# Eight feed-forward modulation chunks: from matmuls to ScalarE scalings summed by adding transfers

## The chip, the core and the metric

The kernel runs on one core of a Trainium2 chip. The metric is the device time of one launch in microseconds; less is better. The kernel before takes 1097.15 us (median of three runs, 1096.75 to 1098.19). A core has TensorE (matmul, PE; its weight loads are PEld), VectorE (DVE), ScalarE (ACT), GpSimd (POOL) and SyncE (SP), each with its own queue of instructions that it runs in order, and 16 DMA engines that move data when one of the queues issues a transfer. They meet at semaphores only.

## The reference

One transformer layer on a sequence of 256 tokens with 2048 features: windowed grouped-query attention with a sink, then a squared-ReLU MLP, each wrapped in an adaptive LayerNorm. What matters here is the modulation: one vector `c` of 2048 numbers gives all shifts, scales and gates.

```python
c_act = jax.nn.silu(c)
mod = c_act @ mod_w[i] + mod_b[i]
sh_m, sc_m, g_m, sh_f, sc_f, g_f = jnp.split(mod, 6, axis=-1)
...
hff = x * (1.0 + sc_f[:, None, :]) + sh_f[:, None, :]
y = sq_relu_mlp(hff, mlp_w1[i], mlp_b1[i], mlp_w2[i], mlp_b2[i])
x = layer_norm(DEEPNORM_ALPHA * x + (1.0 + g_f[:, None, :]) * y, ln_mlp_g[i], ln_mlp_b[i])
```

`c_act @ mod_w` is a vector times a matrix: 2048 x 12288 weights in f32, 100 MB, each used once. Everything is computed to nearly f32 accuracy.

## The kernel before

**Weights.** All large weights come through one stream, class `Stream`. Its list `q` is filled in program order by `S.plan`. Each entry is a load of 128 x 2048 f32 (1 MB) into a buffer called `raw`, issued on SyncE (L202). While attention starts there are eight `raw` buffers; from the second step of the projection loop on there are five (`RAWS`). A load whose buffer is still in use waits at the head of SyncE's queue, and all later loads wait behind it. A matmul weight is split into a high half `wh` (cast by ScalarE, L247) and a low half `wl` (subtraction on VectorE, L218), 1024 columns at a time, five buffers of each. The product is then three matmuls: L498, L499, L500 in the attention part, L971 to L973 in the first feed-forward stage.

**Modulation.** Class `Mod` computes one group of columns of `c_act @ mod_w`. An entry of the stream that belongs to a `Mod` is a chunk, and its work is `Mod.step`. For the feed-forward scale and shift (`m_ff`) there are four groups, 0 to 3, of eight chunks each, 32 chunks in all. A chunk holds two rows of blocks (`k` = 0, 1); each is 128 x 1024, and `cact[:, kt]` has the 128 values of `c_act` that go with its partitions. A chunk is done in one of two ways:

- on TensorE (`quad`, L307): four matmuls side by side in the four column groups of the array, with `c_act` as the weight, f32, 256 columns each, per `k`. They add up in the PSUM tile `pm`, of which there is one.
- on VectorE (`dve`, L343 and L345): multiply by `c_act` and add into an SBUF tile `part` of 128 x 1024. At the end of the group (`Mod.end`) a further `quad` with ones as weights sums `part` over the partitions into the same `pm`.

`Mod.end` then copies `pm` to `mrow` (L361). `columns` transposes `mrow` (L377) to a scale and a shift per feature, and `ff_columns` (L885 to L887) merges them with the LayerNorm's gain. In group 1 chunks 1, 4, 5, 6 are on VectorE, in group 2 chunk 2 alone, in group 3 six of eight; the others are on TensorE.

**Stages.** Around the change: (1) attention by head groups (scores L687 and L693, softmax L702 to L717, transposes L728, values L743) with the output projection (`project`, matmuls L498 to L500, VectorE L803 to L810 and L751 to L753) in a loop of 21 steps; the chunks of `m_ff` 0, 1 and the first two of 2 are mixed in by `SLOT_FILL`. (2) After the last projection the LayerNorm: statistics (L753, L757), `norm_scalars` (L759 to L767), `normed` (L780 on ScalarE, L782 on VectorE), then transposes L901 and the modulated input of the MLP, `ff_input` (L907, L910, L913, L915). `S.vecs(4)` takes four chunks of group 2 here. (3) The first feed-forward stage: 16 steps over `w1a`, with the rest of groups 2 and 3 mixed in by `W1_FILL`; steps 1, 7 and 9 ask for the columns of groups 1, 2 and 3. (4) The other hidden blocks and the output, to the end.

**Order.** A planner (the Tile framework) orders the instructions of every engine: it goes through them by program order as priority, with its own estimate of when inputs arrive, and lets an instruction whose inputs are due pass one whose inputs are not. It also places tiles into buffers and adds all waits. The tile pool `gen` has 20 buffers of 128 x 1024, tag `g4`; `part` comes from there. While `S.behind` is set (stage 1), the first matmul of a `quad` is kept behind the last projection or attention matmul that came before it in the program.

**GpSimd's transfers.** GpSimd issues the broadcast of a bias (`bias_all`, L170), the gate rows (`gate`, L393 and L396) and the loads of `x` (L868).

Of the kernel before, what the change touches and what calls it, by code (L numbers as in the profile page):

```python
# [14 lines left out]
AF = mybir.ActivationFunctionType  # L15
OP = mybir.AluOpType
# [16 lines left out]
FFG = (4, 4, 4, 4)  # L33
# [15 lines left out]
def hybrid_kernel(ctx: ExitStack, tc: tile.TileContext, a, out: bass.AP):  # L49
    nc = tc.nc  # L50
# [23 lines left out]
    def g4(dt=F32):  # L74
        return gen.tile([128, 1024], dt, tag="g4", name="g4")
# [14 lines left out]
    onesf = cst.tile([128, 128], F32, name="onesf")  # L90
# [12 lines left out]
    cact = cst.tile([128, NK], F32, name="cact")  # L103
# [70 lines left out]
    class Stream:  # L174
# [4 lines left out]
        def __init__(self):  # L179
            self.q, self.raw = [], []  # L180
            self.hs, self.ls, self.src = [], [], []
            self.free, self.home, self.used = [raws] * RAWS + [raws2] * MORE, [], 0
            self.of = []
            self.deep = True
            self.at = self.im = 0
            self.nh, self.nl = NHIGH, NLOW
            self.stop = 0
            self.pace = VECS
            self.pin = self.behind = False
            self.prev = None  # L190
            self.side = {}
# [91 lines left out]


    class Mod:
        def __init__(self, srcs, width, dve=(), bias=None):
            self.srcs, self.dve, self.bias = srcs, set(dve), bias
            self.pairs = width == 64
            self.w = 128 if self.pairs else width
            self.kc = 2048 // (4 * width)  # L290
            self.n = NK // self.kc
            self.i = self.planned = 0
            self.whole = len(self.dve) == NK
            self.first = True
            self.part = None
            self.start = -1 if bias is None else max(min(dve) - 1, 0)
# [18 lines left out]
        def step(self, raw):  # L315
            w, kc, i = self.w, self.kc, self.i
            if i == 0 and not self.whole:
                self.ps = psm.tile([128, 512], F32, name="pm")
            r = raw.rearrange("p (k j n) -> p k j n", k=kc // 2 if self.pairs else kc, j=4)
            self.i += 1  # L320
            last = self.i == self.n
            if i == self.start:

                if not self.whole:
                    self.part = [g4() for _ in range(2)]
                for n, p in enumerate(self.part):
                    nc.gpsimd.memset(p, 0.0)
                    nc.scalar.dma_start(p[0:1], self.bias[:, n * 1024:n * 1024 + 1024])
            for k in range(kc):
                kt = i * kc + k  # L330
                if self.pairs:
                    if k % 2 == 0:
                        cols = [cact[:, kt + j // 2:kt + j // 2 + 1].to_broadcast([128, 32]) for j in range(4)]
                        self.quad(cols, [r[:, k // 2, j] for j in range(4)], last and k == kc - 2)
                elif i in self.dve:
                    e = min(4 * w, 1024)
                    new = self.part is None
                    if new:
                        self.part = [g4() for _ in range(4 * w // e)]
                    for n, p in enumerate(self.part):  # L340
                        s = raw[:, k * 4 * w + n * e:k * 4 * w + n * e + e]
                        if new:
                            nc.vector.tensor_scalar(p[:, :e], s, cact[:, kt:kt + 1], None, op0=OP.mult)  # L343
                        else:
                            nc.vector.scalar_tensor_tensor(p[:, :e], s, cact[:, kt:kt + 1], p[:, :e],  # L345
                                                           op0=OP.mult, op1=OP.add)
                else:
                    stop = last and k == kc - 1 and not self.dve
                    self.quad(cact[:, kt:kt + 1].to_broadcast([128, 32]), [r[:, k, j] for j in range(4)], stop)
            if last and not self.whole:  # L350
                self.end()

        def end(self):
            w = self.w
            per = 1024 // w
            if self.dve:
                self.quad(onesf[:, :32], [self.part[j // per][:, (j % per) * w:(j % per) * w + w]
                                          for j in range(4)], True)
            self.r = sml.tile([128, 512], F32, name="mrow", bufs=2)
            if self.bias is None:  # L360
                nc.scalar.copy(self.r[:, :w], self.ps[:, :w])  # L361
            else:
                nc.scalar.activation(self.r, self.ps, AF.Identity, bias=onesf[:, 0:1])
# [32 lines left out]
            nc.gpsimd.dma_start(g[h], row[:, h * 1024:h * 1024 + 1024].partition_broadcast(128))  # L396
        return lambda c: g[c // 2][:, (c % 2) * 512:(c % 2) * 512 + 512]

    def groups(src, sizes, dves):
        out, c0, k0 = [], 0, 0  # L400
        for nk, dve in zip(sizes, dves):
            n = 2 * nk
            out.append((Mod([src[c0 + i] for i in range(n)], 64 * nk, dve), k0, nk))
            c0 += n
            k0 += nk
        return out

    m_mix = groups(a["modm"], MIXG, [(), (), (), (1, 3, 4, 6), (1, 3, 4, 6), (1, 3, 4, 6)])
    m_ff = groups(a["modf"], FFG, [(1, 3, 5, 7), (1, 4, 5, 6), (2,), (1, 2, 4, 5, 6, 7)])
    m_gm = Mod([a["modgm"][i] for i in range(NK)], 512, (1, 3, 5, 6, 8, 9, 11, 12, 14), a["modgmb"])  # L410
    m_gf = Mod([a["modgf"][i] for i in range(NK)], 512, range(NK), a["modgfb"])

# [23 lines left out]
    for g in range(2, G):  # L436
        n = len(ORDER[g])
# [54 lines left out]
    acc, xts, held, xs = {}, {}, {}, [None] * 4  # L492
# [70 lines left out]
    def qkv(g, ch):  # L563

        _, k0, nk = m_mix[g]
        hh, hl = held[g]
        wh, wl = S.main()
        per = 4 // nk
        for ci in range(per):
            p = ch * per + ci  # L570
            c = CORD[p]
            go_on, held_back = c in half, ((g, ch), p) in CARRY
            pss = half.pop(c, None) or banks()
            for k2 in range(0, nk, 2):
                for t in range(NT):
                    for k in (k2, k2 + 1):
                        s = slice(k * 256 + t * 128, k * 256 + t * 128 + 128)
                        mm3(pss[t], hh[:, s], hl[:, s], wh(ci * nk + k), wl(ci * nk + k),
                            k == 0 and not go_on, k == nk - 1 and not held_back)
                S.done()  # L580
                if per == 1 and k2 == 0:
                    yield
            if held_back:
                half[c] = pss
            else:
                evict(c, pss)
            if per == 2 and ci == 0:
                yield
# [195 lines left out]
    def project(j, c):  # L784
        wh, wl = S.main()
        oh, ol = oT[j]
        pss = [psa.tile([128, 512], F32, name="pa") for _ in range(NT)]
        last = j == 3 and c == 3
        for t, rs in [(0, range(4)), (1, range(4))] if last else [(t, (r, r + 1)) for r in (0, 2) for t in range(NT)]:
            for r in rs:  # L790
                s = slice(t * 512 + r * 128, t * 512 + r * 128 + 128)
                mm3(pss[t], oh[:, s], ol[:, s], wh(r), wl(r), r == 0, r == 3)
            if t == 1 or last:
                S.done(not last)
            if last:
                add_gated(pss[t], t, c, g1, st)
                sc.append(norm_scalars(st[t]))
                normed(0, t)
            if t == 1 and rs[0] == 0:
                yield  # L800
        for t, ps in enumerate(pss):
            if j == 0:
                nc.vector.tensor_add(part(ys, t, c), ps, bo(c))  # L803
            elif j < 3:
                y = part(ys, t, c)
                nc.vector.tensor_add(y, y, ps)
                if j == 2:
                    z = part(xs, t, c)
                    nc.vector.tensor_mul(y, y, g1(c))
                    nc.vector.scalar_tensor_tensor(z, z, ALPHA, y, op0=OP.mult, op1=OP.add)  # L810
            elif not last:
                add_gated(ps, t, c, g1, st)
# [21 lines left out]
    for n in range(21):  # L834
        j, i = n // 4, n % 4
# [9 lines left out]
        if n + 1 < len(LATE):  # L845
            w = qkv(*LATE[n + 1])
        else:
            if n == 5:
                ys, bo = [g4b() for _ in range(4)], bias_all(a["bo"], [g4b(), g4b()])
            w = project((n - 5) // 4, (n - 5) % 4)  # L850
# [13 lines left out]
        if n == 9:  # L864

            for c in range(4):
                xs[c] = g4()
                i = nc.gpsimd.dma_start(xs[c].rearrange("p (t n) -> p t n", t=NT), a["x"][:, :, 512 * c:512 * c + 512])  # L868
# [86 lines left out]
    for n, (kg, fq) in enumerate(W1A):  # L955
# [4 lines left out]
        for fp in range(2):  # L960
# [3 lines left out]
            for fi in range(2):  # L964
                o = ps[:, fi * 256:fi * 256 + 256]
                for k in range(4):
                    w = (fp * 2 + fi) * 4 + k
# [208 lines left out]
```

## Time and profile before

| What | Value |
|---|---|
| median of three runs | 1097.15 us |
| the profiled execution's own time | 1100.0 us |
| its span, first to last instruction | 1098.2 us |
| granted clock of TensorE | 0.991 |
| busy: TensorE, VectorE, ScalarE, GpSimd | 1067.6, 804.2, 522.0, 30.0 us |
| DMA queue of SyncE (q1): moved, share of the engines | 279.85 MB, 66.9% |
| DMA queue of GpSimd (q0): moved, share | 10.50 MB, 2.7% |

How to read the lines that follow. A line of a group has the source line, engine, operation, out<-in by the program's names, shapes, and after the bar the busy time, the mean in ns, and the idle time just before with what ended it. A line of the chain has start, length and what ran. Matmuls overlap in the pipeline, so one matmul's duration (392 ns) is longer than its step in a row of them (about 230 ns). An f32 matmul of `quad` is recorded as two instructions.

### The profile page before, as it was taken

To read this page: it belongs to the slowest core of one execution; us is meant where nothing else is said; L and a number is where in the kernel's file an instruction comes from. 1 tells how busy PE (TensorE), PEld (TensorE's weight loads), DVE (VectorE), ACT (ScalarE), POOL (GpSimd) and SP (SyncE) were. 2 spreads that over 40 slices of the span, in tenths; PEclk is the share of its full clock that TensorE was granted. 3 is DMA by queue.
4 is the path that set the end of the run, shared out by engine and by line. 5 is a ranking of instruction groups with operands and counts; after the bars stand their busy time and mean duration, and the time that the engine had idled before them with its cause. 6 is when DMAs were issued, how large, how long until landed. Compare 5 with 4: busy or idle time off the path is not lost.

```text
span 1098.2 us, 15487 instructions
## 1 busy us (share of the span) xinstructions
PE 1067.6 (97%) x6098; PEld 863.1 (79%) x6098; DVE 804.2 (73%) x1162; ACT 522.0 (48%) x806; POOL 30.0 (3%) x54
## 2 busy tenths in 40 slices
PE   8889999998999999999999999999999999999995
PEld 6657677665677799988888888888888888888884
DVE  4597899978899877754588889756666557665676
ACT  5333346765673537643344543344453334544340
POOL 1000000001000000000000010001000000000001
PEclk9989999999999999999999999999999999999998
DMA  9999987789985996555578788866555555557511
GB/s 384 425 427 425 427 357 280 271 297 379 377 315 201 361 360 244 185 192 192 195 301 303 272 313 306 312 220 225 184 189 190 197 196 186 178 185 267 191 75 77
DMA packets 43337, 292.70 MB, mean 267 GB/s; under 512 B 5104, under 2 KB 5232, under 8 KB 9472
## 3 DMA queue, kind: packets, MB, share of 16 engines
q1 hardware_dynamic: 39312, 279.85, 66.9%
q0 software_dynamic: 3200, 10.50, 2.7%
q10 hardware_dynamic: 752, 1.35, 0.3%
q8 instruction: 48, 0.79, 0.3%
q14 instruction: 25, 0.20, 0.0%
HBM read 289.57 MB, written 2.11 MB: 266 GB/s over the span
## 4 chain that ended last, share of the span: by engine, by line
PE 86%; DVE 7%; DMA 4%; ACT 2%; issue 1%; DVEq 0%; ACTq 0%
PE pa L995 16%; PE pa L500 15%; PE pa L498 15%; PE pa L499 15%; PE pa L996 8%; PE pa L972 3%; PE pa L971 3%; PE pa L973 3%; PE pm L307 3%; DVE wl L218 2%; DMA raw<-in_modm 2%; DMA raw<-in_modf 1%; DVE g L345 1%; DMA raw<-in_wqkv 1%; PE pa L687 1%; PE pa L743 1%
## 5 line engine op out<-in xcount | busy, mean ns | idle before, releaser
L218 DVE TENSOR_TENSOR wl<-raw,wh 128x1024 fp32r<-128x1024 f32 x332 | 403.9, 1223 | 223.6 <-ACT wh L247 222.9
L247 ACT CAST wh<-raw 128x1024 fp32r<-128x1024 f32 x332 | 347.1, 1051 | 441.3 <-PE pa L500 228.6
L498 PE MATMUL pa<-wh,g 128*128 128x512 f32 x816 | 324.1, 398 | 5.1 <-ACT g L519 2.6
L500 PE MATMUL pa<-wh,g 128*128 128x512 f32 x816 | 318.9, 392 | 4.1 <-DVE g L521 3.0
L499 PE MATMUL pa<-wl,g 128*128 128x512 f32 x816 | 320.0, 392 | 0.0
L995 PE MATMUL pa<-g,wh 128*128 128x512 f32 x768 | 270.1, 397 | 0.0
L996 PE MATMUL pa<-g,wl 128*128 128x256 f32 x768 | 214.9, 280 | 0.0
L498 PEld LDWEIGHTS pa<-wh,g 128*128 128x128 f32 x816 | 153.9, 189 | 46.8 <-issue 7.5
L500 PEld LDWEIGHTS pa<-wh,g 128*128 128x128 f32 x816 | 153.5, 188 | 41.2 <-DVE g L521 6.0
L499 PEld LDWEIGHTS pa<-wl,g 128*128 128x128 f32 x816 | 153.9, 189 | 33.0 <-issue 2.4
L995 PEld LDWEIGHTS pa<-g,wh 128*128 128x128 f32 x768 | 144.2, 188 | 36.0 <-issue 0.8
L996 PEld LDWEIGHTS pa<-g,wl 128*128 128x128 f32 x768 | 144.8, 189 | 0.1
L345 DVE SCALAR_TENSOR_TENSOR g<-raw,cact,g 128x1024 f32<-128x1024 f32 x65 | 82.6, 1280 | 2.8 <-DMA raw<-in_modf 2.3
L972 PE MATMUL pa<-g,wh 128*128 128x256 f32 x256 | 72.7, 285 | 0.4 <-DVE g L915 0.4
L971 PE MATMUL pa<-g,wh 128*128 128x256 f32 x256 | 72.5, 286 | 0.0
L973 PE MATMUL pa<-g,wl 128*128 128x256 f32 x256 | 72.3, 283 | 0.0
L307 PE MATMUL pm<-raw,cact 128*32 128x256 f32 (+2 forms) x776 | 48.8, 375 | 5.9 <-DMA raw<-in_modf 3.2
L971 PEld LDWEIGHTS pa<-g,wh 128*128 128x128 f32 x256 | 48.8, 192 | 1.3 <-issue 0.8
L972 PEld LDWEIGHTS pa<-g,wh 128*128 128x128 f32 x256 | 49.1, 192 | 0.9 <-DVE g L915 0.8
L973 PEld LDWEIGHTS pa<-g,wl 128*128 128x128 f32 x256 | 49.1, 192 | 0.0
L345 DVE SCALAR_TENSOR_TENSOR g4b<-raw,cact,g4b 128x1024 f32<-128x1024 f32 x32 | 40.7, 1280 | 9.0 <-DMA raw<-in_modgf 8.8
L307 PEld LDWEIGHTS pm<-raw,cact 128*32 128x32 f32 x776 | 20.9, 112 | 25.9 <-issue 11.5
(165 smaller groups left out, 741.6 us busy)
## 6 DMA issues: line engine op xcount, KB each, us to landing
raw<-in_w SPq DMA_DIRECT2D x64, 1024.0 KB, 4.9
raw<-in_w1b SPq DMA_DIRECT2D x48, 1024.0 KB, 5.0
raw<-in_modm SPq DMA_DIRECT2D x32, 1024.0 KB, 14.8
raw<-in_modf SPq DMA_DIRECT2D x32, 1024.0 KB, 6.9
raw<-in_wqkv SPq DMA_DIRECT2D x24, 1024.0 KB, 12.8
raw<-in_modgm SPq DMA_DIRECT2D x16, 1024.0 KB, 7.5
raw<-in_wo SPq DMA_DIRECT2D x16, 1024.0 KB, 7.5
raw<-in_w1a SPq DMA_DIRECT2D x16, 1024.0 KB, 7.6
```

Of the source, the lines that this page charges most:

```text
L218: self.pinned(nc.vector.tensor_sub(l, r, f32(self.hs[n])))
L247: self.pinned(nc.scalar.copy(h, s))
L307: i = nc.tensor.matmul(self.ps[32 * j:32 * j + 32, :w], lhsT[j] if type(lhsT) is list else lhsT, rhs[j], start=self.first, stop=stop)
L345: nc.vector.scalar_tensor_tensor(p[:, :e], s, cact[:, kt:kt + 1], p[:, :e], op0=OP.mult, op1=OP.add)
L498: nc.tensor.matmul(ps, xh, wh, start=start, stop=False)
L499: nc.tensor.matmul(ps, xh, wl, start=False, stop=False)
L500: S.prev = nc.tensor.matmul(ps, xl, wh, start=False, stop=stop).ins
L971: nc.tensor.matmul(o, wh(w, 128), hh, start=new, stop=False)
L972: nc.tensor.matmul(o, wh(w, 128), hl, start=False, stop=False)
L973: nc.tensor.matmul(o, wl(w, 128), hh, start=False, stop=end)
L995: nc.tensor.matmul(ps, wh(k, 128), hb, start=k == 0, stop=False)
L996: nc.tensor.matmul(ps[:, :256], wl(k, 128), hb[:, :256], start=False, stop=k == NK - 1)
```

## The change

Beside `dve`, a group can now have a set `acc` of chunks. For such a chunk ScalarE multiplies each 128 x 1024 half by its `c_act` column. The first half of a group goes into a new SBUF tile `sum` (from `gen`). Every later one is scaled in place in its `raw` buffer, and GpSimd issues a transfer from `raw` to `sum` that adds to what is there. At the end of the group one more `quad` with ones sums `sum` over the partitions into `pm`. Group 1's chunks 0, 2, 3 and group 2's chunks 0, 1, 3, 4, 5 are done so: eight chunks, sixteen halves, fourteen transfers. They were all on TensorE before. Group 1 keeps chunk 7 on TensorE, group 2 keeps 6 and 7.

```diff
-        def __init__(self, srcs, width, dve=(), bias=None):
-            self.srcs, self.dve, self.bias = srcs, set(dve), bias
+        def __init__(self, srcs, width, dve=(), bias=None, acc=()):
+            self.srcs, self.dve, self.bias, self.acc = srcs, set(dve), bias, set(acc)
+            self.sum = None
...
+                elif i in self.acc:
+
+                    s = raw[:, k * 1024:k * 1024 + 1024]
+                    if self.sum is None:
+                        self.sum = g4()
+                        nc.scalar.activation(self.sum, s, AF.Copy, scale=cact[:, kt:kt + 1])
+                    else:
+                        nc.scalar.activation(s, s, AF.Copy, scale=cact[:, kt:kt + 1])
+                        nc.gpsimd.dma_start(self.sum, s, accum_op=OP.add)
...
-                    stop = last and k == kc - 1 and not self.dve
+                    stop = last and k == kc - 1 and not self.dve and not self.acc
...
-                                          for j in range(4)], True)
+                                          for j in range(4)], not self.acc)
+            if self.acc:
+                self.quad(onesf[:, :32], [self.sum[:, j * w:j * w + w] for j in range(4)], True)
...
-    def groups(src, sizes, dves):
+    def groups(src, sizes, dves, accs=((),) * 8):
...
-    m_ff = groups(a["modf"], FFG, [(1, 3, 5, 7), (1, 4, 5, 6), (2,), (1, 2, 4, 5, 6, 7)])
+    m_ff = groups(a["modf"], FFG, [(1, 3, 5, 7), (1, 4, 5, 6), (2,), (1, 2, 4, 5, 6, 7)],
+                  [(), (0, 2, 3), (0, 1, 3, 4, 5), ()])
```

More of the change, by code (lines that the diff above doesn't have):

```diff
@@ L397, in gate @@
         return lambda c: g[c // 2][:, (c % 2) * 512:(c % 2) * 512 + 512]
-    def groups(src, sizes, dves):
+    def groups(src, sizes, dves, accs=((),) * 8):
         out, c0, k0 = [], 0, 0
-        for nk, dve in zip(sizes, dves):
+        for nk, dve, acc in zip(sizes, dves, accs):
             n = 2 * nk
-            out.append((Mod([src[c0 + i] for i in range(n)], 64 * nk, dve), k0, nk))
+            out.append((Mod([src[c0 + i] for i in range(n)], 64 * nk, dve, acc=acc), k0, nk))
             c0 += n
```

## The prediction

> **What bounds the kernel now.** I read the page first (busy times, then the chain that ended last), then the stages around the changed chunks.
>
> ```profile
> PE 1067.6 (97%) x6098; PEld 863.1 (79%) x6098; DVE 804.2 (73%) x1162; ACT 522.0 (48%) x806; POOL 30.0 (3%) x54
> PE 86%; DVE 7%; DMA 4%; ACT 2%; issue 1%; DVEq 0%; ACTq 0%
> ```
>
> TensorE holds 86% of the chain, so work taken off it counts, where it is really the last to finish. The table by stretch (columns: us; busy and instructions of PE, PEld, DVE, ACT, POOL; granted clock; DMA share and GB/s) follows the feed-forward chunks through the attention and projection stage (281 to 358.3), the LayerNorm gap (358.3 to 366.5) and the first feed-forward stage.
>
> ```profile
> 281.00:300.00 19.00, 18.98 (x134) 12.26 (x135) 16.30 (x32) 14.78 (x37) 0.00 (x0) 1.00 0.92 357
> 300.00:320.00 20.00, 20.00 (x134) 13.56 (x130) 19.80 (x42) 14.26 (x37) 1.10 (x2) 1.00 0.91 347
> 320.00:340.00 20.00, 20.00 (x109) 14.54 (x106) 17.34 (x32) 11.14 (x23) 0.00 (x0) 1.00 0.64 245
> 340.00:358.30 18.30, 18.30 (x82) 15.08 (x82) 17.56 (x25) 5.44 (x6) 0.00 (x0) 1.00 0.48 172
> 358.30:366.50 8.20, 7.07 (x99) 3.52 (x97) 6.96 (x29) 2.65 (x6) 0.00 (x0) 1.00 0.83 296
> 366.50:415.00 48.50, 48.10 (x413) 45.54 (x410) 38.22 (x51) 24.86 (x35) 0.00 (x0) 1.00 0.96 384
> 281.00:358.30 77.30, 77.28 (x450) 55.42 (x449) 70.99 (x130) 45.62 (x101) 1.10 (x2) 1.00 0.74 282
> ```
>
> From 281 to 358.3 TensorE is busy without a break, VectorE is close behind (70.99 of 77.30), ScalarE has 31.7 us free. The DMA engines are nearly full until 320 and half idle after it. In the gap TensorE is not the bound; after it, it is again.
>
> **What is removed.** Count the groups of feed-forward modulation from 0. Group 1's chunks 0, 2, 3 and group 2's 0, 1, 3, 4, 5 leave TensorE. The chain shows what one chunk costs there (x16 is one chunk: two halves of four matmuls, each recorded twice; the x24 is chunk 7 of group 1 with the closing sum over `part`).
>
> ```profile
> 281.90 1.00 PE pm L307 x16
> 287.86 1.00 PE pm L307 x16
> 292.86 1.00 PE pm L307 x16
> 311.15 1.43 PE pm L307 x24
> 316.36 1.00 PE pm L307 x16
> 338.95 1.00 PE pm L307 x16
> ```
>
> Chunks 0, 2, 3 of group 1 and 0, 1 of group 2 stand at 281.90, 287.86, 292.86, 316.36 and 338.95: five times 1.00, all on the path, -5.00 us. The x24 prices a closing sum: 1.43 - 1.00 = 0.43 us. The other three chunks of group 2 run in the gap:
>
> ```profile
> 357.15 1.14 DVE wl L218
> 358.31 4.93 DMA raw<-in_modf
> 363.28 1.05 PE pm L307 x10
> 364.33 0.37 PE pt L901 x2
> 364.69 0.57 PE pm L307 x8
> 365.26 0.49 PE pt L901 x3
> 365.78 0.57 ACT g L907
> ```
>
> There the chain is VectorE, then the load of the last chunk of group 2, then the transposes L901, which need the normalised rows anyway. Three chunks more or less on TensorE before 363.28 change nothing: 0. An earlier load could give up to the 1.05 that stands before the transposes; I take 0, as they also need the LayerNorm chain.
>
> **What is added on TensorE.** A second closing sum in each of the two groups, 0.43 each. Group 1's is on the path (+0.43). Group 2's follows the last chunk around the transposes (+0.43).
>
> **What is added on ScalarE.** Sixteen scalings of 128x1024: two write the sum, fourteen work in place. The nearest rows, of ScalarE over the stage and of the end:
>
> ```profile
> L247 ACT CAST wh<-raw 128x1024 fp32r<-128x1024 f32 x17 | 17.7, 1050 | 19.3 <-PE pa L500 12.0 <-DVE g L752 7.2
> L717 ACT ACTIVATE g<-g,rs 128x256 f32<-128x256 f32 x20 | 8.6, 505 | 1.0 <-DVE rs L711 1.0
> L1080 ACT ACTIVATE g<-g,r 128x512 f32<-128x512 f32 x2 | 1.4, 723 | 5.5 <-DVE r L767 5.5
> ```
>
> L717 and L1080 are the same operation with a scale per partition: 505 ns at 256 columns, 723 at 512, so 218 per 256, and 723 + 436 = 1.16 us at 1024 (the cast's 1.05 is the other end). Sixteen make 18.6 us. If fourteen fall into the stage (16.2), they lie in its 31.7 free, in pieces: the casts L247 had waited 12.0 us for buffers that TensorE frees, so a cast 1.16 us late still is ahead. I charge 0. Without that cover, a cast that TensorE waits for would cost up to 1.16 per scaling.
>
> **What is added on GpSimd and the DMA engines.** Fourteen transfers from SBUF into SBUF that add, 512 KB each, five for group 1 and nine for group 2. Each waits for its scaling and, since all of a group write one tile, for the transfer before it. GpSimd's issues of this size cost 0.55 us, 7.7 in all, on an engine busy 1.10 us of the stage. Queued on GpSimd with them are the loads of x ahead and two bias loads, which are first used in the feed-forward output. The trace has no transfer that adds. The nearest are GpSimd's 512 KB loads:
>
> ```profile
> L170 POOL DMA_DIRECT2D g4b<-in_b x2: 547/548/549, 311.4 to 319.3; - x2
> DMA to landing us min/median/max: 4.3/5.5/6.8
> L396 POOL DMA_DIRECT2D g4b<-row x4: 532/547/562, 245.5 to 748.4; - x4
> DMA to landing us min/median/max: 4.3/6.6/8.7
> g<-in_x POOLq DMA_DIRECT2D x4, 512.0 KB, 11.1
> ```
>
> The ends are 4.3 and 8.7 (11.1 where four stand in one queue); I take 5.5, as most of group 2's run after 320, where the share falls to 0.64 and 0.48. Group 1: five make 27 us. Its chunk 0 can be scaled when it lands, not when TensorE reaches it: the loads from 264.20 below. Done by about 305, before its closing sum at 312 less what is saved: hidden, 0. Group 2 is tighter:
>
> ```profile
> 264.20 10.10 SPq L202 DMA_DIRECT2D raw<-in_modf  x3
> 332.78 8.87 SPq L202 DMA_DIRECT2D raw<-in_modf  x4
> DMA to landing us min/median/max: 4.7/5.7/7.7
> ```
>
> The four from 332.78 are its chunks 3 to 6 (the landing row is of SyncE's loads in the stage). With 3.57 us saved by then, chunk 3 is issued at 329.2, lands at 334.9, is scaled at 336.1, and six transfers follow in a row: with 5.5 they end at 369.1. The closing sum can wait, because the planner orders each engine by when inputs are due, and its columns are asked for only at step 7 of the first feed-forward stage; I price it at 0 and the other case as a rival. The Trainium skill ("DMA: Bandwidth & Descriptors", section "Anatomy of one DMA — SWDGE (gpsimd) path") gives such a transfer about 2.0 us plus bytes over 436 GB/s. That would be 3.2 us here, the six would end at 355 and the rival below would fall away; the rows, all 4.3 and above, do not agree.
>
> **A raw buffer is now held** until its second transfer has landed, not until TensorE has read it. Five buffers serve all loads, and SyncE's queue stands still behind a load whose buffer is not free. Chunks that ScalarE takes when they land start their holding earlier, so I charge 0, with 0 to 13 us as bounds (third rival).
>
> **VectorE as the next bound.** If TensorE needs 77.30 - 4.57 = 72.73, VectorE's 70.99 fill 98% of it. Where they already touched:
>
> ```profile
> PEld pa L498 <- DVE g L345: 0.8, 1, 0.8
> PEld pa L498 <- DVE wl L218: 0.3, 1, 0.3
> ```
>
> That is 1.1 us in the stage before; I charge as much again, +1.1, with 0 and 4.57 (everything taken) as the ends.
>
> **The sum.** -5.00 + 0.43 + 0.43 + 1.1 = -3.0 us. The profiled execution took 1100.0 us (span 1098.2), so it would take 1097.0. It stood 2.85 above the median of 1097.15; against that median the forecast is 1094.1. Its own range is 1091.6 (no VectorE loss, and the 1.05 before the transposes won) to 1095.5.
>
> **Rivals.**
> 1. VectorE takes the gain. The four windows of the stage show 1.0, the third 2.7 us free; if the order of its work keeps the 6.3 idle us that it has, nothing is won and the closing sum remains: 1097.15 + 0.43 = 1097.6. For it speaks 19.80 of 20 us from 300 to 320; against it, that the high and low halves are made several buffers ahead of TensorE.
> 2. Slower, by one wait: the closing sum of group 2 stands in TensorE's order before the transposes of the gap while its transfers still run. Its place is 364.69 less the 4.6 saved, 360.1. Six transfers from 336.1 reach it if each takes more than 4.0 us. At 4.3 it waits 1.8; at 5.5, 9.0, which makes 1094.1 + 9.0 = 1103.1; at 6.6, 15.6. Against it: nothing needs this sum for another 40 us, so it is placed there only if the planner takes the transfers for shorter than they are.
> 3. The adding transfers slow the weight loads. At 357 GB/s for a share of 0.92 a full load is 388 GB/s; one add occupies the engines 1.35 us if its 0.52 MB count once, 2.7 if twice. Six before 320 are 8 to 16 us, where 3.3 are free, so loads come 5 to 13 us later; the 17 us free after 320 then take up the rest. If the cover of casts ahead is 5 us short, the sum is 1094.1 + 5 = 1099.1 and, at the far end, 1102. The Trainium skill ("Collectives: The Full Stack", section "The bandwidth ceiling: the fold count and why AG ≠ RS ≠ AR") says that an add in a transfer needs two source reads on one ring, which halved the rate there. That speaks for the 2.7 and against the change; no run here shows it yet.
>
> **How the numbers follow.** 0.2% of 1097 is 2.2 us, about what can be told from no change. The forecast 0.50, of which 0.02 falls within 2.2; VectorE 0.15 (no difference); the wait at the closing sum 0.22 (slower); the loads 0.13 (slower). Faster 0.48, same 0.17, slower 0.35. The range runs from 1091.6 to 1103.1, which leaves out the waits over 9 us and the far end of the loads, under 2 in 10.
>
> **What would show it.** L307 on TensorE: 128 instructions fewer, 16 more on the sum. Between 281 and the end of the projection TensorE without gaps and about 4.5 us shorter. Sixteen scalings of about 1.16 us, most right after their loads land. Fourteen transfers on GpSimd, 4.3 to 6.6 us each, one after another. No wait of TensorE for a transfer at a closing sum. The gap after the projection as long as before. I am wrong if TensorE idles before the closing sum of group 2 (rival 2), if casts wait for loads (rival 3), or if VectorE is busy throughout and TensorE waits for L218 and L345 (rival 1).

## The result and the profile after

The changed kernel takes 1154.43 us (median of four runs, 1151.84 to 1157.42) against 1096.95 (1096.12 to 1098.19) of the kernel before beside it: a ratio of 1.0523, 95% interval 1.0498 to 1.0548. It is 5% slower, where 1094.1 was forecast. The profiled execution took 1151.84 us with a span of 1150.1, 51.9 us more than before. The two profiled executions differ already ahead of the change: TensorE's closing sum of group 0, which comes before the first scaling, stands at 269.99 after and at 274.00 before, a lead of 4.0 us. From there to the end the changed kernel takes 55.9 us more (880.1 against 824.2). In the changed kernel `quad` is L308, the scalings are L341 and L343, the adding transfers L344, VectorE's `dve` L353 and L355, the projection's matmuls L511 to L513, the first feed-forward matmuls L984 to L986, and the transposes of the normalised rows L914.

From the page after: busy times, the chain by engine, GpSimd's DMA queue, and the group of `quad`.

```profile
PE 1066.8 (93%) x5986; PEld 862.8 (75%) x5986; DVE 804.0 (70%) x1162; ACT 538.9 (47%) x822; POOL 42.3 (4%) x68
PE 61%; DMA 2%; DVE 2%; issue 1%; ACT 1%; DVEq 0%; ACTq 0%; SPq 0%
q0 software_dynamic: 5216, 17.85, 5.9%
L308 PE MATMUL pm<-raw,cact 128*32 128x256 f32 (+2 forms) x648 | 42.4, 390 | 33.6 <-DMA raw<-in_modf 30.1
```

TensorE fell from 97% to 93% of a longer span, and its busy time hardly moved (1067.6 to 1066.8), although 112 matmul instructions net are gone. The chunks that are left on it have idle time before them that ends with transfers. TensorE's own order of work around the stage shows three holes (columns: start, length, what ran, and in brackets the idle time before it with what ended it):

```profile
328.19 1.93 PE L308 MATMUL pm<-raw,cact 128*32 128x256 f32 x16 [18.57 <-DMA raw<-in_modf]
...
377.40 1.07 PE L308 MATMUL pm<-raw,cact 128*32 128x256 f32 x16
388.31 1.93 PE L308 MATMUL pm<-raw,cact 128*32 128x256 f32 x16 [9.84 <-DMA raw<-in_modf]
390.01 1.08 PE L308 MATMUL pm<-g,onesf 128*32 128x256 f32 x8
409.76 1.08 PE L308 MATMUL pm<-g,onesf 128*32 128x256 f32 x8 [18.66 <-DMA g<-raw]
```

The first is the last chunk of group 1, which waits 18.57 us for its load. The second is chunk 7 of group 2, 9.84 us for its load. The third is the new closing sum of group 2 (weights `onesf`): the first closing sum, over `part`, runs at 390.01; the second waits 18.66 us for the last adding transfer. Together 47.07 us.

Why the loads are late shows in SyncE's issues, together with the transfers L344. Chunk 7's load of group 1 is issued here:

```profile
322.69 0.99 SPq L202 DMA_DIRECT2D raw<-in_modf  x2
```

It goes out as the second transfer of chunk 3 lands (issued at 317.39, landed 5.2 us later, at 322.6), so the buffer that it waited for was that of chunk 3. In group 2 it is the same: a transfer lands at 377.7, the loads that wanted its buffer go out from 377.86, chunk 7's at 378.28. How long the fourteen transfers take, over the whole kernel, and the end of the chain at the closing sum:

```profile
L344 POOL DMA_DIRECT2D g<-raw x14: 861/868/917, 280.7 to 405.3; - x14
DMA to landing us min/median/max: 4.4/7.0/10.9
```
```profile
389.10 4.45 DMA g<-raw
...
393.69 5.83 DMA raw<-in_w1a
...
405.30 4.41 DMA g<-raw
409.71 0.04 issue
409.76 1.13 PE pm L308 x8
```

The fourteen times from issue to landing, in order, are 10.8, 8.5, 5.0, 10.2, 5.2 for group 1 and 10.1, 5.3, 4.7, 10.9, 5.5, 10.2, 4.5, 10.7, 4.4 for group 2: two kinds, 4.4 to 5.5 and 8.5 to 10.9. The two kinds mostly alternate, and the lines say why. A chunk's second transfer lands at 393.55 (389.10 + 4.45) and frees a `raw` buffer. SyncE issues loads at once (393.69, 394.11 and 394.59). The next adding transfer goes out at 394.1 beside them and takes 10.7. Its successor at 405.30 has only the last half MB of these loads beside it and takes 4.41. Beside the quick transfers 0 to 1.1 MB of loads moved, beside the slow ones 1.7 to 2.6 MB. So the transfers hold back the loads, and the loads that they release slow the next transfer.

The table by stretch gives the clock in and after each hole.

```profile
309.20:328.20 19.00, 0.43 (x4) 0.01 (x2) 7.44 (x17) 3.92 (x11) 1.43 (x2) 0.60 0.84 247
328.20:332.60 4.40, 4.40 (x26) 3.01 (x27) 0.00 (x0) 1.13 (x3) 0.00 (x0) 0.50 1.01 387
378.10:388.30 10.20, 0.37 (x8) 0.00 (x0) 3.70 (x6) 1.99 (x2) 0.87 (x1) 0.66 0.88 257
388.30:390.40 2.10, 2.09 (x20) 0.99 (x24) 2.08 (x8) 0.00 (x0) 0.87 (x1) 0.50 0.00 0
390.50:409.70 19.20, 0.59 (x8) 0.00 (x0) 2.19 (x11) 2.62 (x4) 1.74 (x2) 0.59 0.87 246
409.70:418.00 8.30, 6.06 (x36) 3.05 (x36) 4.18 (x11) 4.27 (x7) 0.00 (x0) 0.50 0.87 333
```

After each hole the granted clock is 0.50: 4.40, 2.09 and 6.06 us of work, which at the full clock would be half as long, so up to 6.3 us more. Holes and slow clock make at most 47.1 + 6.3 = 53.4 of the 55.9 us counted from the closing sum of group 0; what is left, 2.5, is small waits less the removed chunks. In the holes the DMA share is 0.84 to 0.88, yet they move 246 to 257 GB/s, against 347 to 357 at a share of 0.91 to 0.92 in the stretches 281 to 320 before the change.

### The profile page after: what moved, and what is told of

Its sections match the earlier page's. It is cut to its first block, busy times and chain, and to the rows that moved or that the text cites. A ratio compares the mean times of both kernels' runs of the same rounds, so it can differ in the third digit from the quotient of the medians.

```text
span 1150.1 us, 15315 instructions
## 1 busy us (share of the span) xinstructions
PE 1066.8 (93%) x5986; PEld 862.8 (75%) x5986; DVE 804.0 (70%) x1162; ACT 538.9 (47%) x822; POOL 42.3 (4%) x68
## 4 chain that ended last, share of the span: by engine, by line
PE 61%; DMA 2%; DVE 2%; issue 1%; ACT 1%; DVEq 0%; ACTq 0%; SPq 0%
PE pa L1008 16%; PE pa L511 10%; PE pa L512 10%; PE pa L513 10%; PE pa L1009 8%; PE pa L984 2%; PE pa L985 2%; PE pa L986 2%; DMA raw<-in_modf 1%; DMA g<-raw 1%; DMA raw<-in_w1a 1%; DVE g L355 0%; DVE wl L218 0%; PE pt L914 0%; ACT wh L247 0%
## 5 line engine op out<-in xcount | busy, mean ns | idle before, releaser
L218 DVE TENSOR_TENSOR wl<-raw,wh 128x1024 fp32r<-128x1024 f32 x332 | 404.0, 1222 | 254.5 <-ACT wh L247 252.9
L511 PE MATMUL pa<-wh,g 128*128 128x512 f32 x816 | 323.5, 397 | 8.0 <-ACT g L532 3.1
L513 PE MATMUL pa<-wh,g 128*128 128x512 f32 x816 | 318.2, 392 | 3.2 <-DVE g L534 2.0
L511 PEld LDWEIGHTS pa<-wh,g 128*128 128x128 f32 x816 | 153.4, 188 | 49.9 <-issue 7.1
L513 PEld LDWEIGHTS pa<-wh,g 128*128 128x128 f32 x816 | 153.1, 188 | 41.2 <-DVE g L534 5.3
L355 DVE SCALAR_TENSOR_TENSOR g<-raw,cact,g 128x1024 f32<-128x1024 f32 x65 | 82.5, 1278 | 9.1 <-DMA raw<-in_modf 8.8
L308 PE MATMUL pm<-raw,cact 128*32 128x256 f32 (+2 forms) x648 | 42.4, 390 | 33.6 <-DMA raw<-in_modf 30.1
L984 PE MATMUL pa<-g,wh 128*128 128x256 f32 x256 | 73.3, 290 | 0.0
L986 PE MATMUL pa<-g,wl 128*128 128x256 f32 x256 | 73.1, 286 | 0.0
L308 PEld LDWEIGHTS pm<-raw,cact 128*32 128x32 f32 x648 | 17.9, 116 | 51.2 <-DMA raw<-in_modf 31.3
L984 PEld LDWEIGHTS pa<-g,wh 128*128 128x128 f32 x256 | 49.8, 196 | 1.2 <-issue 0.8
L986 PEld LDWEIGHTS pa<-g,wl 128*128 128x128 f32 x256 | 49.9, 195 | 0.0
L355 DVE SCALAR_TENSOR_TENSOR g4b<-raw,cact,g4b 128x1024 f32<-128x1024 f32 x32 | 40.7, 1280 | 8.1 <-DMA raw<-in_modgf 7.8
```

The source lines that it names most:

```text
L218: self.pinned(nc.vector.tensor_sub(l, r, f32(self.hs[n])))
L308: i = nc.tensor.matmul(self.ps[32 * j:32 * j + 32, :w], lhsT[j] if type(lhsT) is list else lhsT, rhs[j], start=self.first, stop=stop)
L511: nc.tensor.matmul(ps, xh, wh, start=start, stop=False)
L513: S.prev = nc.tensor.matmul(ps, xl, wh, start=False, stop=stop).ins
L984: nc.tensor.matmul(o, wh(w, 128), hh, start=new, stop=False)
L986: nc.tensor.matmul(o, wl(w, 128), hh, start=False, stop=end)
```

## The experiments

All ratios are to the kernel before, run on the same chip.

**The scalings without the transfers.** What is the rest of the change worth?

```diff
-                        nc.gpsimd.dma_start(self.sum, s, accum_op=OP.add)
```

> The sixteen scalings stay on ScalarE, the fourteen transfers are left out, so the sums of groups 1 and 2 hold only their first half chunk; the second closing sums stay. If the loss of 57 us comes from the transfers (held raw buffers, the wait at the closing sum, or DMA time), it is gone whole: 1097 less the 3.0 of the forecast, 1092 to 1096. If it comes from ScalarE, whose casts come late behind the scalings, or from the planner's new order, most of it stays: 1120 or more. If VectorE takes what TensorE gives up, 1096 to 1098.

Measured: 1098.41 us against 1096.56 (ten runs), 1.0024 (1.0011 to 1.0037). All of the loss is gone with the fourteen transfers, but no gain appears. TensorE's order of work shows where it went; first this kernel, then the kernel before:

```profile
272.37 0.64 PE L308 MATMUL pm<-g,onesf 128*32 128x256 f32 x8
...
354.77 0.38 PE L388 MATMUL pt<-ident,mrow 128*128 128x128 f32 x2
...
366.10 1.22 PE L983 MATMUL pa<-g,wh 128*128 128x256 f32 x4
```
```profile
274.00 0.64 PE L307 MATMUL pm<-g,onesf 128*32 128x256 f32 x8
...
358.18 0.38 PE L377 MATMUL pt<-ident,mrow 128*128 128x128 f32 x2
...
366.56 0.50 PE L971 MATMUL pa<-g,wh 128*128 128x256 f32 x2
```

The projection ends 3.41 us earlier (354.77 against 358.18), the feed-forward stage starts only 0.46 earlier: the gap is 11.3 us instead of 8.4. But 1.63 of the 3.41 is a lead that this execution has before the change can act, at the closing sum of group 0 (272.37 against 274.00). From there the stage is only 1.78 us shorter up to the end of the projection, and 1.17 us longer up to the feed-forward stage, which fits the medians (1.85 us slower). The table rows of the two stretches up to the end of the projection (the kernel before comes first), and then TensorE's two waits in this kernel with ScalarE's work ahead of the second:

```profile
274.00:358.18 84.18, 84.17 (x486) 59.28 (x487) 75.80 (x139) 50.47 (x113) 1.10 (x2) 1.00 0.76 294
272.37:354.77 82.40, 80.37 (x414) 57.67 (x415) 74.76 (x140) 66.83 (x131) 1.09 (x2) 1.00 0.89 343
```
```profile
285.82 1.13 PE L699 MATMUL pa<-g,g 64*128 64x256 f32 x8 [0.72 <-ACT g L680]
291.98 2.25 ACT L343 ACTIVATE raw<-raw,cact 128x1024 f32<-128x1024 f32 x2
294.07 1.12 ACT L742 COPY g<-pt 128x512 f32<-128x512 f32 x2
294.76 1.94 PE L755 MATMUL pa<-g,g 128*64 128x512 f32 x8 [1.23 <-ACT g L742]
```

TensorE's busy time falls by 3.80 us, and 2.03 us of idle time come in. Of these, 1.95 are waits for ScalarE's copies of transposed rows; the copy L742 stands directly behind two scalings. VectorE's lines of this kernel in the gap:

```profile
358.37 1.22 DVE L218 TENSOR_TENSOR wl<-raw,wh 128x1024 fp32r<-128x1024 f32 x1
...
360.07 1.22 DVE L218 TENSOR_TENSOR wl<-raw,wh 128x1024 fp32r<-128x1024 f32 x1
```

With chunks leaving their buffers sooner, feed-forward weights are there before the LayerNorm is done, and two low halves of 1.22 us stand among its small steps, on which the transposes wait.

**The same, with the low halves behind the LayerNorm.** Does the gain come back?

```diff
+            i = nc.vector.tensor_sub(l, r, f32(self.hs[n]))
+            self.pinned(i)
+            if self.norm is not None and 82 <= n < 86:
+                tc.add_manual_dep(i.ins, self.norm.name, ORDER_ONLY, reason="after the norm")
...
+        if g == 0:
+            S.norm = last.ins
```

> As e1 (scalings alone, the adds left out), and the four low halves of the second and third weights of the first feed-forward stage are ordered on VectorE behind the first input of that stage. In e1 TensorE was 3.4 us early at the end of the projection and lost 3.3 in the gap, where three subtractions L218 of 1.2 us stood between the steps of the LayerNorm on VectorE. If they took the gain, this gives 1093 to 1095; if the gap is set by something else, it stays within 1 us of e1.

Measured: 1095.33 against 1095.77 (twelve runs), 0.9993 (0.9976 to 1.0010). In its profile the first feed-forward matmul starts at 360.64, 5.9 us before that of the kernel before, but its profiled execution (1093.76 us) is below its own median, and 4.4 of the 5.9 us stand already at the closing sum of group 0 (269.58 against 274.00). From there to the first feed-forward matmul it takes 91.06 us against 92.56, and its gap is 8.8 us instead of the 11.3 of the version before. Over twelve runs no difference is left that can be told from none. So with the transfers free of charge, and the order repaired, the saving is worth at most some 0.2%.

**Scaling into a buffer of its own.** If the held `raw` buffers are the cause, this takes it away: the load's buffer is free after the scaling, and the transfer reads another tile.

```diff
-                        nc.scalar.activation(s, s, AF.Copy, scale=cact[:, kt:kt + 1])
-                        nc.gpsimd.dma_start(self.sum, s, accum_op=OP.add)
+                        v = g4()
+                        nc.scalar.activation(v, s, AF.Copy, scale=cact[:, kt:kt + 1])
+                        nc.gpsimd.dma_start(self.sum, v, accum_op=OP.add)
```

> ScalarE writes the scaled half into an SBUF tile of its own (from gen) and the transfer adds from there, so a raw buffer is free when ScalarE has read it. Number, size and chain of the transfers are the same. If raw buffers held by the transfers are what stops the loads, the two waits of TensorE for a load of a modulation chunk (18.7 and 10.2 us) go and the wait at the closing sum of group 2 stays, shorter or longer with the chain: 1110 to 1127. If the DMA time of the adds is what delays the loads, those waits stay: over 1140.

Measured: 1142.88, 1.0437 (1.0413 to 1.0461). Its waits over 260 to 415 us (columns here and below: total, times, longest):

```profile
PEld pm L308 <- DMA g<-g: 28.5, 2, 27.9
...
PEld pa L757 <- ACT g L744: 11.6, 2, 11.3
```

TensorE's waits for loads are gone, and only 11.5 of the 57.5 us with them, so neither case of the forecast fits. The closing sum now waits 27.9 us. And a scaling on ScalarE waits 9.7 us for a `gen` buffer that a transfer holds, with the copy L744 of a transpose behind it in ScalarE's queue, on which TensorE waits 11.3. The last transfer still lands only at 402.3 (409.7 in the changed kernel); the chain is felt elsewhere.

**A transfer that reads nothing that anyone waits for.** The transfers add a constant tile of zeros, so that neither `raw` nor a scaled tile is held by them.

```diff
-                        self.sum = g4()
+                        self.sum, self.fix = g4(), g4()
+                        nc.gpsimd.memset(self.fix, 0.0)
...
-                        nc.gpsimd.dma_start(self.sum, s, accum_op=OP.add)
+                        nc.gpsimd.dma_start(self.sum, self.fix, accum_op=OP.add)
```

> All fourteen transfers add, in the same chain, but from one fixed SBUF tile of zeros in place of the raw buffer, so no raw buffer waits for a transfer (the scaled halves after the first are dropped; the sums hold the first half only). If the held raw buffers stop the loads, TensorE's two waits for a load of a modulation chunk (18.7 and 10.2 us) go, and what remains is the wait at the closing sum of group 2: 1100 to 1122. If the DMA time of the adds delays the loads whoever holds what, the waits stay: over 1140.

Measured: 1140.07, 1.0398 (1.0364 to 1.0433).

```profile
PEld pm L308 <- DMA g<-g: 34.8, 2, 20.7
```

No matmul waits more than 1.6 us for a load, and now both groups wait at their closing sum (14.2 us, up to 333.1, and 20.7, up to 401.8). The time is that of the second case, the waits are those of the first: neither forecast held. Some 13 of the 57.5 us are gone. Freeing the buffers is not enough: five and nine transfers in a row are too long for each group.

**The closing sums moved to where the columns are asked for.** If only the place of the closing sum were at fault, this would repair it: it runs in `columns`, in a PSUM tile of its own.

```diff
-                                          for j in range(4)], not self.acc)
-            if self.acc:
-                self.quad(onesf[:, :32], [self.sum[:, j * w:j * w + w] for j in range(4)], True)
+                                          for j in range(4)], True)
...
+        if m.acc:
+            late = pst.tile([128, 512], F32, name="pt")
+            for j in range(4):
+                nc.tensor.matmul(late[32 * j:32 * j + 32, :m.w], onesf[:, :32], m.sum[:, j * m.w:j * m.w + m.w],
+                                 start=True, stop=True)
+            nc.vector.tensor_add(r[:, :m.w], r[:, :m.w], late[:, :m.w])
```

> The changed kernel whole, with only the closing sums moved as in e9; the transfers read the raw buffers and hold them. If the waits for held buffers stand by themselves, the 19.3 us at the closing sum of group 2 go and the 18.7 and 10.2 us for loads stay: 1125 to 1137. If both are the same chain seen at two places, the waits for loads grow by what the closing sum gives up and the time stays over 1145.

Measured: 1145.03, 1.0448 (1.0414 to 1.0481).

```profile
PE pm L308 <- DMA raw<-in_modf: 43.5, 3, 17.6
```

No closing sum waits, and the waits for loads rise from 28.4 to 43.5 us (17.6, 12.1 and 13.8 at three chunks): 15 of the 19 us of the closing sum are found again at the held buffers. The time lies on the border of the second case, and some 9 of the 57.5 us are gone. One chain of transfers, two places where it can be felt.

**Both: zeros as the source, and late closing sums.** Then no load waits for a buffer that a transfer holds, and no matmul of the stage waits for the sum. What is left is the transfers' time on the DMA engines (and whatever else the edit brings).

> As e5 (the fourteen transfers add from a fixed tile of zeros, so no raw buffer is held; the sums hold the first half only), and the closing sums over the added tiles move: they go to a PSUM tile of their own when the columns of the group are asked for, in the first feed-forward stage, so TensorE's order has them about 50 us after where they stood. All transfers with their DMA time are still there. If the loss is only the two waits, for held buffers and at the closing sums, it is gone: 1096 to 1104. If the DMA time of the adds costs by itself, 1115 or more.

Measured: 1120.26, 1.0218 (1.0192 to 1.0244): some 33 of the 57.5 us are gone, 24 are left. The table by stretch, and two waits:

```profile
281.00:300.00 19.00, 15.43 (x82) 10.46 (x82) 13.64 (x32) 15.77 (x35) 1.30 (x2) 1.00 1.00 335
300.00:320.00 20.00, 19.76 (x109) 12.76 (x108) 19.86 (x43) 14.79 (x34) 1.73 (x2) 1.00 1.02 369
...
340.00:360.00 20.00, 20.00 (x90) 15.68 (x87) 18.17 (x27) 10.53 (x11) 1.72 (x2) 1.00 1.03 354
```
```profile
ACT g L720 <- issue: 11.7, 1, 11.7
...
PE pm L308 <- DMA raw<-in_modf: 6.4, 3, 6.0
```

The DMA share is 1.00 and 1.02 up to 320 and 1.03 from 340, where it was 0.92, 0.91 and 0.48 before. Chunk 7 of group 2 waits 6.0 us for its load again, though no transfer holds its buffer: it went out at 358.90, and the chunk could start at 372.4 only. A further 6.4 us of TensorE's waiting (behind L720) probably belongs to the test itself: L720 starts at 329.0, just when the last transfer of group 1 lands, so it seems to wait for a buffer of `gen` that the zeros occupy until then. So the 24 us aren't all the DMA engines', and how they divide stays open.

**A plain copy in place of the add.** The bytes, the order and the buffers held stay the same; only what a transfer does with each byte differs.

```diff
-                        nc.gpsimd.dma_start(self.sum, s, accum_op=OP.add)
+                        nc.gpsimd.dma_start(self.sum, s)
```

> The transfers copy instead of adding (the sum then holds only the last half chunk); waits, chain and buffers are the same. If the second source read of an add is the price, a transfer falls from 4.4 to 3 us alone and from 10 to 6 beside loads, and the time falls by half of the loss or more, under 1125. If the fixed part of a transfer and the loads beside it are the price, it falls by less than a third: over 1135.

Measured: 1135.87, 1.0373 (1.0350 to 1.0397). GpSimd's queue, its issues and their landing:

```profile
q0 software_dynamic: 5216, 17.85, 4.3%
```
```profile
L344 POOL DMA_DIRECT2D g<-raw x14: 528/528/549, 282.3 to 391.3; - x14
DMA to landing us min/median/max: 2.8/6.1/9.6
```

The price of an add follows from three shares of q0, each of its own span. Before: 2.7% of 1098.2 = 29.7 us. Changed kernel: 5.9% of 1150.1 = 67.9, so the fourteen adds took 38.2, or 2.7 us each of all 16 engines. Plain copies: 4.3% of 1133.8 = 48.8, so 19.1, or 1.4 us each. An add costs the engines twice a copy of the same 0.52 MB. At its quickest it also lands 1.6 us later (4.4 against 2.8), and its issue occupies GpSimd 0.87 us instead of 0.53. But the copy keeps two thirds of the loss, just inside the second case: waits of 12.9 and 5.2 us for loads and 13.9 at the closing sum. The larger part is fourteen transfers in a chain, whatever they do.

**Two sums.** Halving the chain: the two halves of a chunk go to two tiles, `self.sums[k]`, with one more closing sum each.

```diff
-                        nc.gpsimd.dma_start(self.sum, s, accum_op=OP.add)
+                        nc.gpsimd.dma_start(self.sums[k], s, accum_op=OP.add)
...
-                self.quad(onesf[:, :32], [self.sum[:, j * w:j * w + w] for j in range(4)], True)
+                for n, q in enumerate(self.sums):
+                    self.quad(onesf[:, :32], [q[:, j * w:j * w + w] for j in range(4)], n == 1)
```

> The first halves are added into one tile and the second halves into another (one closing sum more per group, 0.43 us each), so the two transfers of a chunk may run side by side and a chain has half the links. If the length of the chain is the price, the loss halves: 1115 to 1130. If it is the DMA time of the adds, a transfer in a pair takes twice as long and the loss stays: over 1140.

Measured: 1131.10, 1.0316 (1.0278 to 1.0354). The twelve transfers land after 4.5 to 13.2 us (median 8.6), longer each, as two of them now often run side by side. The closing sum waits 2.4 us only, but chunk 7 of group 2 still waits 15.5 for its load. Shorter, and not short enough: 35 of the 57.5 us are left, a little more than the forecast half.

**Fewer chunks.** First group 1 alone (five transfers), then chunk 0 of group 1 and chunks 0, 1 of group 2 (four transfers).

```diff
-                  [(), (0, 2, 3), (0, 1, 3, 4, 5), ()])
+                  [(), (0, 2, 3), (), ()])
```

> Only group 1's chunks 0, 2, 3 go to ScalarE and the transfers; group 2 is on TensorE as before. If each group's waits are its own, what stays is the wait of 18.7 us for the load behind chunk 3 of group 1, less 2.6 saved on TensorE: 1110 to 1116. If that wait can be taken up later, where loads have room, 1097 to 1105.

```diff
-                  [(), (0, 2, 3), (0, 1, 3, 4, 5), ()])
+                  [(), (0,), (0, 1), ()])
```

> Only chunk 0 of group 1 and chunks 0 and 1 of group 2 go this way: one transfer and three, where the chain has time before its closing sum (30 us and 40 us). TensorE is spared 3.00 less two closing sums, 2.1 us. If a chain that fits is free, 1093.5 to 1096; if a held buffer costs even so, 1098 to 1106.

Measured: 1120.49, 1.0233 (1.0201 to 1.0264), and 1108.56 (six runs), 1.0113 (1.0090 to 1.0135). Waits of the first from 300 to 330 us, and of the second from 260 to 415:

```profile
PEld pm L308 <- DMA raw<-in_modf: 17.9, 1, 17.9
```
```profile
DVE g L355 <- DMA raw<-in_modf: 7.9, 2, 6.7
PEld pa L513 <- DVE g L759: 7.4, 2, 4.3
```

Group 1 alone makes the first hole as it was; it isn't made up in the gap or later. The loss of 24 us is 6 more than the hole and lies 4 us above the forecast; smaller waits of 0.7 to 1.9 us for ScalarE and VectorE between 281 and 302 and a clock of 0.54 after the hole are seen beside it, but not priced. Four transfers, three of them after 320, where the DMA engines were half idle before, still cost 1.1%, 2.6 us above the forecast for a held buffer. Loads come 6.7 us late to VectorE's `dve` at 294.10 and 4.6 us late at 339.00, and the output sums L759 queued behind them on VectorE keep TensorE waiting 3.1 us from 301.9 and 4.3 from 340.9.

**The add on GpSimd itself.** No transfer at all; the chain of sums stays.

```diff
-                        nc.gpsimd.dma_start(self.sum, s, accum_op=OP.add)
+                        nc.gpsimd.tensor_add(self.sum, self.sum, s)
```

> No transfers: GpSimd adds the scaled half to the sum itself, fourteen additions of 128x1024. From the one addition of 128x512 in the kernel before (1.75 us) each takes about 3.4 us, 6.8 for a chunk, beside no load and with no landing to wait for. If the transfers' time in the chain is the cause, nearly all of the loss goes: 1095 to 1102, as e1 with 1098.4. If GpSimd's additions slow VectorE down, over 1105.

Measured: 1121.08, 1.0215 (1.0187 to 1.0244). TensorE no longer waits for a load or for a closing sum; it waits 3.4 to 4.9 us four times for VectorE. VectorE's groups from 281 to 360 (columns: busy, mean ns, then idle before), and the same step in the kernel before over 281 to 358:

```profile
L218 DVE TENSOR_TENSOR wl<-raw,wh 128x1024 fp32r<-128x1024 f32 x14 | 24.4, 1739 | 0.6 <-ACT wh L247 0.5
...
L765 DVE TENSOR_TENSOR g<-g,tmp 128x512 f32<-128x512 f32 x3 | 6.2, 2091 | 0.0
L764 DVE TENSOR_TENSOR tmp<-pa,g4b 128x512 f32<-128x512 f32 x4 | 2.6, 676 | 0.0
```
```profile
L752 DVE TENSOR_TENSOR g<-g,tmp 128x512 f32<-128x512 f32 x6 | 4.0, 684 | 0.0
```

The GpSimd adds take 2.4 to 3.3 us each. A VectorE operation with both inputs in SBUF (L765, L218) grows beside them, 684 to 2091 ns and 1219 to 1739; L764, which reads one input from PSUM, keeps its 676. The Trainium skill ("SBUF — State Buffer", section "Who interferes with whom") says that a VectorE instruction with two SBUF inputs contends with a GpSimd instruction that reads SBUF. These three rows agree.

None of the eleven versions beats the kernel before.

## Why the prediction was wrong

**TensorE's saving: half of it came, and the match of the sum is luck.** -5.00 + 0.43 + 1.1 by the end of the projection is -3.47; without the transfers the projection ended 3.41 us earlier. But 1.63 of that is a difference between two executions ahead of the change; from the closing sum of group 0 on it is 1.78. The busy time fell by 3.80 of the forecast 4.57, and the idle time that came in is ScalarE's, not the 1.1 us charged for VectorE.

**ScalarE: right in size, wrong as a wait.** 1.16 us for a scaling was forecast, and 1.17 is the mean of the fourteen in place. It was charged 0 because casts have room to be late. But the attention's copies stand in the same queue, and without the transfers TensorE waits 0.72 and 1.23 us for two of them, where before no matmul in this stretch waited for ScalarE. That the scalings cause the second wait is read from the order of ScalarE's work; no run took them away alone.

**The gap charged 0: wrong, and small.** Where loads come earlier the gap grows, from 8.4 to 11.3 us, by low halves that VectorE takes in among the LayerNorm's steps. The text named VectorE as the next bound and priced it at 1.1 us up to the projection; the 2.9 us in the gap was missing. With the low halves ordered behind the LayerNorm the gap was 8.8 us again. With these 2.9 us the forecast of a faster kernel would have failed even with transfers at no cost.

**The transfer's price, 5.5 us: the first failing term.** Only the far bound of 11.1 (several in one queue) held all fourteen (4.4 to 10.9). Their mean is 7.6 (106 us in sum), and six lie above 10, beyond the 8.7. The choice of 5.5 rested on a DMA share of 0.64 and 0.48 after 320, taken from the kernel before. In the changed kernel the landing of a chunk's second transfer releases loads, so the next add meets a full queue. The estimate of 3.2 us that the prediction makes from the Trainium skill ("DMA: Bandwidth & Descriptors", section "Anatomy of one DMA — SWDGE (gpsimd) path") is lower still; no add came below 4.4.

**The raw buffer, "I charge 0": the step that failed outright.** It cost 18.57 and 9.84 us. The bounds were 0 to 13, and the sentence that chunks start their holding earlier missed how long the hold is. A chunk's buffer is held through two transfers that stand in the same chain as all others of the group. Group 1's chunk 3 is the fourth and fifth of five, at 306.62 and 317.39, and its buffer came free at 322.6 where TensorE had nothing left to do without chunk 7 at 309.6. The price of one transfer was multiplied by the length of the chain for the closing sum, and not for the buffers.

**The closing sum "priced at 0": rival 2's mechanism, undersized.** The planner did put it before the transposes, and it waited 18.66 us. The rival gave 9.0 at 5.5 us per transfer and 15.6 at 6.6. Its first transfer was taken to go out at 336.1 and the sixth to end at 369.1; the trace has 360.8 and 409.7: 24.7 us later to begin with, by the first hole and by the chunks before in the same chain, and 48.9 us long instead of 33. The rival also took the wait as one that could stand alone; the runs with own buffers and with late closing sums show that the same chain is felt at the buffers as soon as it isn't felt there.

**Rival 3: right in kind.** An add takes the engines 2.7 us, twice a copy: the "counted twice" of that rival, and the rule of two source reads from the Trainium skill's "Collectives: The Full Stack" (section "The bandwidth ceiling: the fold count and why AG ≠ RS ≠ AR") fits the 2.7 against 1.4. With a plain copy 18.6 of the 57.5 us are gone (1154.4 to 1135.9). Its end of 1102 was too low, as it had the late loads without the held buffers.

**Rival 1** did not decide in the changed kernel: four small waits of 0.9 to 1.2 us for VectorE and ScalarE end between 292 and 302, beside holes of ten and nineteen. Without the transfers its outcome, no gain, is the nearest of the four (1.0024), though by ScalarE's copies in the stage and by VectorE in the gap. Its reading of the room on VectorE was off: the four windows leave 2.7, 0.2, 2.7 and 0.7 us. The low end of the forecast's own range does not follow from its terms either: 1097.15 - 5.00 + 0.86 - 1.05 is 1092.0, not 1091.6.

In sum: the sum treated three effects of one chain as three separate terms, each hidden. The waits that were removed one at a time came back at the other place; removing both left 24 us, of which the DMA engines' time is a part that these runs don't separate fully.

## What to carry to other kernels

Price a chain of transfers into one tile as a chain: its length is the number of members times the time from issue to landing under the load that the change itself releases, and everything that a member holds (source buffers, their next loads, the reader of the sum) is late by that length. When a stage has a queue of loads behind a few buffers, ask of each buffer when its last reader ends, not when its main reader does. And a saving of 5 us on TensorE was worth nothing here even without the transfers: look at the order of work on the other engines, in the stage and in the gap behind it. When two profiles are compared, compare them from a point ahead of the change; here three executions led that of the kernel before by 1.6 to 4.4 us there.

## What the runs showed of the hardware

- An accumulating SBUF-to-SBUF transfer of 512 KB takes 2.7 us of all 16 DMA engines, a plain one 1.4; at their quickest they land after 4.4 and 2.8 us, and GpSimd's issue takes 0.87 and 0.53 us.
- The accumulating transfer lands after 4.4 to 5.5 us where at most 1.1 MB of loads move beside it, and after 8.5 to 10.9 us where 1.7 to 2.6 MB do.
- After idle times of 10 and 19 us TensorE ran at a granted clock of 0.50 in the stretches of 2.1 to 8.3 us that were looked at: a chunk of `quad` took 1.93 us instead of 1.07. The three holes cost up to 6.3 us more than their length.
- A GpSimd add of 128 x 1024 slows VectorE's operations with two SBUF inputs up to threefold (L765: 0.68 to 2.09 us in the mean), and leaves L764, with one PSUM input, as it is (0.68).
